# Attention scores as fp32 products of two heads side by side, in place of split float32r products

## The chip, the cores and the metric

The kernel runs on one core of one Trainium2 chip. The metric is the device time of one execution in microseconds, the median of three runs. TensorE, VectorE, ScalarE, GpSimd and SyncE are called PE, DVE, ACT, POOL and SP in the profile's rows; PEld is the weight load of PE.

## The reference

Two layers of a transformer trunk, on one sequence of 256 tokens with 1024 channels. Each layer takes shift, scale and gate from a condition vector, normalises, mixes, and adds the gated result to x. All matrices are float32.

```python
for i in range(2):
    shift, scale, gate = split(cond @ ada_w[i] + ada_b[i], 3)
    h = rms_norm(x, norm_g[i]) * (1 + scale) + shift
    x = x + gate * (nsa_mixer if i == 0 else moba_mixer)(h, ...)

# both mixers: 16 query heads of 64 channels, 4 key/value heads ("key groups"); query head h uses group h // 4
q, k.. = partial_rope(rms_norm(..., g))          # per head
# layer A (nsa): three attentions with the same q, each with keys of its own, mixed by per-head gates
o = g0 * softmax(q @ k_cmp.T * s) @ v_cmp        # 15 compressed keys a group
  + g1 * softmax(q @ k_sel.T * s) @ v_sel        # 256 tokens: at this length all blocks are selected
  + g2 * softmax(q @ k_win.T * s) @ v_win        # 256 tokens: at this length the window holds them all
# layer B (moba): one causal attention over 256 tokens
o = softmax(q @ k.T * s) @ v
return (o * silu(z)) @ w_out
```

## The kernel before, in words

**Products.** A float32 matrix that meets another in a large product is split in two float32r parts, `hi` (a rounding copy on ACT) and `lo` (a subtraction on DVE), and the product is the three matmuls hi·hi, hi·lo, lo·hi. This is done for the normalised input (`HT`), every projection weight (`parts_of`, tags `hi` and `lo`), and the gated attention output (`GT`, tag `qg`). The projections run in chunks of 512 columns: `piece` loads a quarter of the rows (128 partitions x 2 x 512) by one DMA on SP's queue into a `raw` buffer, `parts_of` splits it, `product` issues the matmuls. `z_blocks` does the same with the weight as the stationary side, so that the gate branch z comes out transposed.

**Scores.** They too were split. `make_k` normalises and rotates the keys, copies each head twice beside itself on ACT (`twice`, tag `y`), transposes the four key groups, and splits the transposed keys into `KTA[:, 0]` (hi) and `KTA[:, 1]` (lo). So each of the two parts has the 64 channels twice on its 128 partitions. `make_q` puts the hi and lo part of a head beside each other (`n_parts`), transposes that as float32r, and copies it to the query tile (`qg`): 64 partitions hi, 64 partitions lo. A score is then two matmuls with 128 contraction rows, against the hi keys and against the lo keys.

**Attention.** `pair_a(i)` and `pair_b(i)` handle two neighbouring heads, `e` = 0 and 1, that use one key group. For layer A a pair has three score blocks of 256 columns (tokens 0 to 127 against both kinds of keys, tokens 128 to 255 against each), for layer B one of 128 and one of 256 columns. DVE masks a block and takes the row maximum (`masked_top`), ACT takes the exponential with its sum (`exps`), DVE scales, PE transposes the probabilities (`p_transposed`), and `values` forms the outputs with two heads side by side in the columns of PE: 128 x 64 tiles, plain fp32 operands. `compressed(hf)` handles eight heads against 16 compressed keys each. Plain fp32 matmuls show as two records each in the trace.

**Tiles of PE.** A matmul with `tile_position` uses a part of the array. In the kernel before these are the 128 x 32 tiles of the condition products (`condz`), the 128 x 64 tiles of `values` and of the compression, the 32 x 128 tiles of `Vbd`, and one pair of 64 x 128 tiles, in `ada_gate(0)` (tile `row` against `ones`).

**Order.** Nothing is issued as it is written. Each engine call is recorded with an estimated duration, a tile pool and a level, and `Plan.issue` then simulates the engines and emits the calls engine by engine: the earliest call that can start, ties by level and by number. Numbers are moved by a table, `LATER_BY`; starts are held back by another, `HOLD`. `Plan._safe` says whether a tile may be taken ahead of its turn, `Plan._rank` prefers calls that keep PE in a tiled form. PSUM has eight banks: two `acc` and six `ps`; scores, transposes and outputs of the attention use `ps`. The projections of z in layer A, and the output products of a layer, are issued between the steps of the attention.

Of the kernel before, what the change touches and what calls it, by code (L numbers as in the profile page):

```python
# [9 lines left out]
F32 = mybir.dt.float32  # L10
# [47 lines left out]
    29: 2400, 32: 3700, 33: 3700, 51: 7200, 312: 35600, 391: 48800, 1276: 152700, 1340: 169100, 1350: 168000,  # L58
    1415: 182100, 1573: 197400, 1576: 198800, 1579: 197400, 1585: 198700, 1636: 205200, 1655: 209300,
# [13 lines left out]
class Plan:  # L73
# [120 lines left out]
    def _cost(self, engine, method, args, kw, aps):  # L194
# [15 lines left out]
        if engine == "T":  # L210
# [3 lines left out]
            if aps[2].dtype == F32:  # L214
                m, rows = free(aps[1]), aps[1].shape[0]
                if "tile_position" in kw and m * rows <= 64 * P:
                    return max(cols * 4.28 * max(32, m) / P * max(32, rows) / P, 60.0) + (100.0 if rows < P else 0.0)
# [25 lines left out]
    def _rank(op, e, mode):  # L243

        if e == "T" and op["level"] >= 0 and op["mode"] and mode:
            return TILED
# [1294 lines left out]
```

## Time and profile before

| | before |
|---|---|
| median of 3 runs | 312.29 us (312.12 to 313.19) |
| the profiled execution, its time | 312.48 us |
| its span | 310.7 us |
| PE busy | 301.6 us, 97% |
| PEld busy | 242.0 us, 78% |
| DVE busy | 242.0 us, 78% |
| ACT busy | 205.1 us, 66% |
| moved by DMA | 65.82 MB, mean 212 GB/s |

A matmul's record lasts from its start to the end of its pipeline, so neighbouring records overlap and the busy share is above what the array computes. What a matmul costs its neighbours is read from start to start. In a row of the timeline the first number is the start, the second the length of the whole row, and "x16" is the number of records merged in it; a row's cost is thus the next row's start minus its own. In a table of stages the columns are busy microseconds and records of PE, PEld, DVE, ACT and POOL, then PE's granted clock (1.00 is full), the DMA share and GB/s.

### The profile page before, as it was taken

The page shows a single profiled execution, that of the slowest core. Times are in us where ns is not written, and L with a number is a line of the kernel's source. Part 1 is how long each engine was busy: PE and PEld are TensorE (multiplying, and loading weights), DVE is VectorE, ACT ScalarE, POOL GpSimd, SP SyncE. Part 2 cuts the span into 40 slices and gives each one's busy share as a digit, 9 for nine tenths or more (in the row PEclk, how much of TensorE's full clock was granted, in tenths as well). Part 3 has the DMA queues.
Part 4 walks back from the last instruction along what each step waited for, and adds up shares of the span by engine and source line. Part 5 has one row for each costly group of instructions (what it writes and reads, how often), then busy time and mean ns, then how long its engine had stood idle before and what let it go on. Part 6 is the DMA issues. An engine that isn't in the chain of part 4 may idle for free.

```text
span 310.7 us, 6167 instructions
## 1 busy us (share of the span) xinstructions
PE 301.6 (97%) x2133; PEld 242.0 (78%) x2133; DVE 242.0 (78%) x734; ACT 205.1 (66%) x486; POOL 28.2 (9%) x99
## 2 busy tenths in 40 slices
PE   4999999999999999999999999999999999999995
PEld 4765677768767687976798887787788999987784
DVE  4763483658997399963999989796799999999465
ACT  4735254784845566964999993795585599988520
POOL 8038950000000000000000000000000000000000
PEclk9999999999999999999999999999999999999999
DMA  8999999749999890948925429236288760740002
GB/s 249 321 356 368 366 356 319 223 139 307 331 294 333 282 345 6 329 145 290 309 80 186 153 72 307 96 77 198 69 289 273 225 231 9 263 136 2 0 35 103
DMA packets 44174, 65.82 MB, mean 212 GB/s; under 512 B 4221, under 2 KB 20971, under 8 KB 44142
## 3 DMA queue, kind: packets, MB, share of 16 engines
q1 hardware_dynamic: 43782, 65.36, 64.3%
q8 instruction: 17, 0.28, 0.4%
q14 instruction: 15, 0.12, 0.1%
q10 hardware_dynamic: 168, 0.06, 0.1%
q0 software_dynamic: 192, 0.00, 0.0%
HBM read 64.36 MB, written 1.05 MB: 211 GB/s over the span
## 4 chain that ended last, share of the span: by engine, by line
PE 90%; DVE 3%; DMA 3%; ACT 2%; issue 1%; ACTq 0%; SPq 0%; DVEq 0%
PE ps L404 52%; PE acc L404 38%; DMA y<-in_ada_b_dram 2%; DMA early<-in_nsa_w_in_dram 1%; ACT hi L404 1%; DVE lo L404 1%; DVE rs L404 1%; DVE y L404 0%; ACT n_parts L404 0%; ACTq L404 0%; DVE X L404 0%; DVE p L404 0%; ACT n_out L404 0%; ACT HT L404 0%; DVE n_parts L404 0%
## 5 line engine op out<-in xcount | busy, mean ns | idle before, releaser
L404 ACT CAST hi<-raw 128x1024 fp32r<-128x1024 f32 (+1 forms) x48 | 48.6, 1021 | 24.3 <-PE acc L404 16.5
L404 DVE TENSOR_TENSOR lo<-raw,hi 128x1024 fp32r<-128x1024 f32 (+1 forms) x48 | 56.5, 1182 | 6.5 <-ACT hi L404 6.3
L404 PE MATMUL acc<-hi,HT 128*128 128x512 f32 (+1 forms) x160 | 49.6, 382 | 0.1
L404 ACT ACTIVATE p<-p,tiny 128x128 f32<-128x128 f32 (+1 forms) x96 | 42.9, 451 | 6.5 <-DVE tiny L404 6.2
L404 PE MATMUL acc<-HT,hi 128*128 128x256 f32 x192 | 37.4, 285 | 0.0
L404 DVE CUSTOM_DVE_ANT_0 p<-ps,causal 128x128 f32<-128x128 f32 (+1 forms) x96 | 30.6, 346 | 8.2 <-ACT hi L404 5.6
L404 PEld LDWEIGHTS acc<-hi,HT 128*128 128x128 f32 x160 | 29.1, 188 | 8.0 <-issue 2.5
L404 PEld LDWEIGHTS acc<-HT,hi 128*128 128x128 f32 x192 | 30.2, 189 | 0.5 <-issue 0.5
L404 PE MATMUL acc<-lo,HT 128*128 128x512 f32 (+1 forms) x80 | 30.3, 383 | 0.2
L404 PE MATMUL ps<-hi,HT 128*128 128x512 f32 (+1 forms) x96 | 28.2, 365 | 0.0
L404 PE MATMUL acc<-HT,lo 128*128 128x256 f32 x96 | 27.2, 284 | 0.0
L404 PE MATMUL ps<-KTA,qg 128*128 128x256 f32 (+2 forms) x192 | 26.9, 281 | 0.0
L404 PEld LDWEIGHTS ps<-KTA,qg 128*128 128x128 f32 x192 | 24.0, 189 | 2.7 <-issue 1.7
L404 ACT COPY pT<-ps 128x384 f32<-128x384 f32 x48 | 21.0, 477 | 4.0 <-PE ps L404 4.0
L404 ACT CAST hi<-early 128x1024 fp32r<-128x1024 f32 (+2 forms) x17 | 14.9, 896 | 13.1 <-DMA early<-in_nsa_w_in_dram 8.9
L404 PE MATMUL ps<-hi,qg 128*128 128x256 f32 (+1 forms) x96 | 23.4, 326 | 0.0
L404 DVE TENSOR_TENSOR lo<-early,hi 128x1024 fp32r<-128x1024 f32 (+2 forms) x17 | 17.6, 1047 | 5.9 <-ACT hi L404 5.9
L404 PE MATMUL acc<-hi,qg 128*128 128x512 f32 x64 | 21.7, 405 | 0.0
L404 PE MATMUL ps<-identF,p 128*128 128x128 f32 x144 | 21.2, 274 | 0.0
L404 PEld LDWEIGHTS ps<-hi,HT 128*128 128x128 f32 x96 | 17.0, 188 | 3.5 <-issue 1.2
L404 PEld LDWEIGHTS ps<-identF,p 128*128 128x128 f32 x144 | 16.8, 141 | 2.7 <-issue 0.7
L404 PE MATMUL ps<-pT,VA 128*64 128x256 f32 (+1 forms) x192 | 18.5, 333 | 0.0
(220 smaller groups left out, 614.4 us busy)
## 6 DMA issues: line engine op xcount, KB each, us to landing
raw<-in_ada_w_dram SPq DMA_DIRECT2D x32, 512.0 KB, 5.2
raw<-in_moba_w_in_dram SPq DMA_DIRECT2D x20, 512.0 KB, 4.4
early<-in_ada_w_dram SPq DMA_DIRECT2D x12, 512.0 KB, 9.5
raw<-in_nsa_w_in_dram SPq DMA_DIRECT2D x12, 512.0 KB, 6.8
early<-in_nsa_w_in_dram SPq DMA_DIRECT2D x9, 512.0 KB, 8.8
p<-in_nsa_cmp_w_dram SPq DMA_DIRECT2D x16, 256.0 KB, 4.1
raw<-in_nsa_w_out_dram SPq DMA_DIRECT2D x8, 512.0 KB, 4.8
raw<-in_moba_w_out_dram SPq DMA_DIRECT2D x8, 512.0 KB, 5.2
```

The lines of the kernel that those rows point to most:

```text
L404: r = getattr(self.engines[e], method)(*[self._real(a) for a in args], **{k: self._real(a) for k, a in kw.items()})
```

## The change

Queries and keys stay fp32 and have no low parts. The transposed key tile holds two key groups, one on partitions 0 to 63 and one on 64 to 127 (`KTA` is `[P, 2, 528]` fp32 in place of `[P, 2, 4, 528]` float32r), and the transposed query tile holds one head of each of these groups in the same way (tag `q`, two tiles). A score is one fp32 matmul with 64 contraction rows; the two heads of a pair stand one above the other in 64 x 128 tiles of PE and write two PSUM banks. So a pair's heads come from two key groups (heads j and j + 4 of a half of eight), and what goes by head is put in that order: the query projection's copies (`by_head`, `raw_part`), the gates, the z weights (`parts_of` with `paired`), the rows of the output weights (`out_piece`, two DMAs of 64 partitions in place of one of 128), the compressed values.

```diff
@@ scores
-        s = tile_of("ps", 2, 256)
-        with plan.group(need):
-            for e in range(2):
-                T.matmul(s[:, e, 0:n], q[e], kt[:, 0, g, k0:k0 + n], start=(e == 0), stop=False)
-                T.matmul(s[:, e, 0:n], q[e], kt[:, 1, g, k0:k0 + n], start=False, stop=(e == 1))
+        s = [tile_of("ps", sum(n for _, _, n in spans)) for e in range(2)]
+        at = 0
+        with plan.group(*needs):
+            for b, (m, k0, n) in enumerate(spans):
+                for e in range(2):
+                    half = slice(64 * e, 64 * e + 64)
+                    T.matmul(s[e][:, at:at + n], QT[i // 4][half, i % 4, m * P:(m + 1) * P], kt[half, i // 4, k0:k0 + n],
+                             start=(b == 0), stop=(b == len(spans) - 1), tile_position=(64 * e, 0))
+                at += n
@@ pair_a: scores(i, KTA, ((0, 128, 256),), p) and scores(i, KTA, ((1, 256, 256), (1, 0, 256)), *two)
@@ pair_b: scores(i, KTB, ((0, 0, P), (1, 0, S)), *pm)
@@ make_k
-            twice = tile_of("y", KVH, 2 * HD)
-            A.copy(twice.rearrange("p g (a d) -> p g a d", a=2),
-                   y[:, 4 * j:4 * j + 4, None, :].to_broadcast([P, KVH, 2, HD]))
-            t = tile_of("ps", 512)
+            t = tile_of("ps", 2, P)
             with plan.group():
-                for g in range(KVH):
-                    T.transpose(t[:, g * P:(g + 1) * P], twice[:, g], identF)
...
-            A.copy(hi, tv)
-            V.tensor_sub(lo, tv, hi.bitcast(F32))
+                for hf in range(2):
+                    T.transpose(t[:, hf], y[:, 4 * j + 2 * hf:4 * j + 2 * hf + 2].rearrange("p e d -> p (e d)"), identF)
+            A.copy(kt_view[:, :, off:off + P], t)
@@ make_q
-            qs = tile_of("n_parts", 8, 2, HD)
-            src = y[:, 8 * m:8 * m + 8]
-            A.copy(qs[:, :, 0, :], src)
-            V.tensor_sub(qs[:, :, 1, :], src, qs[:, :, 0, :].bitcast(F32))
-            for gg in range(2):
...
-                        T.transpose(t.bitcast(F32R)[:, h * P:(h + 1) * P],
-                                    qs[:, 4 * gg + h].rearrange("p a d -> p (a d)"), identR)
-                A.copy(qt[g0 + gg][:, :, m * P:(m + 1) * P], t.rearrange("p (h k) -> p h k", h=4))
+            t = tile_of("ps", 512)
+            with plan.group():
+                for h in range(4):
+                    T.transpose(t[:, h * P:(h + 1) * P],
+                                y[:, 8 * m + 2 * h:8 * m + 2 * h + 2].rearrange("p e d -> p (e d)"), identF)
+            A.copy(qt[g0 // 2][:, :, m * P:(m + 1) * P], t.rearrange("p (h k) -> p h k", h=4))
@@ compressed
-        s = tile_of("ps", 2, 8, 2, 16)
+        s = [tile_of("ps", 2, 4, 16) for e in range(2)]
...
-                    T.matmul(s[:, m, h], QT[g][:, h % 4, m * P:(m + 1) * P], KTA[:, :, g, 512:528],
-                             start=(m == 0 and h == 0), stop=(m == 1 and h == 7))
+                    half = slice(64 * (h % 2), 64 * (h % 2) + 64)
+                    T.matmul(s[h % 2][:, m, h // 2], QT[hf][half, h // 2, m * P:(m + 1) * P],
+                             KTA[half, hf, 512:528], start=(m == 0 and h < 2), stop=(m == 1 and h >= 6),
+                             tile_position=(64 * (h % 2), 0))
...
-        V.tensor_add(pc, s[:, :, :, 1], maskC[:, :, None, :].to_broadcast([P, 2, 8, 16]))
-        V.tensor_add(pc, s[:, :, :, 0], pc)
+        for e in range(2):
+            V.tensor_add(pc[:, :, e::2], s[e], maskC[:, :, None, :].to_broadcast([P, 2, 4, 16]))
@@ out_piece (new, in place of piece for the output weights)
+        with plan.at(CHAIN):
+            for e in range(2):
+                Q.dma_start(t[64 * e:64 * e + 64], bass.AP(tensor=w.tensor, offset=w.offset + (512 * hf + 256 * e + 64 * j) * D + c0,
+                                                           ap=[[D, 64], [64 * D, KP], [1, n]]))
@@ parts_of, paired (for z_blocks)
+                t = t.rearrange("p k (e j d) -> p (k e) j d", e=2, d=HD)
+                hv, lv = (h.rearrange("p k n -> p (k n)").rearrange("p (j c d) -> p c j d", j=4, d=HD) for h in (hi, lo))
@@ pools
-    plan.tag("n_parts", work, 1024, 2, F32R)
+    plan.tag("n_parts", work, 1024, 4, F32R)
-    ATTN = {"qg": (1024, 5, F32R), "zT": (512, 4, F32), "p": (512, 6, F32),
+    ATTN = {"qg": (1024, 4, F32R), "q": (1024, 2, F32), "zT": (512, 4, F32), "p": (512, 6, F32),
@@ first_parts: weight quarters of layer B's first chunk that are split before layer A ends
-        for kp in range(4):
+        for kp in range(3):
@@ Plan
-        if e == "T" and op["level"] >= 0 and op["mode"] and mode:
+        if e == "T" and op["level"] >= 0 and op["mode"] and mode == op["mode"]:
@@ LATER_BY: other numbers (63 entries before, 46 now); HOLD: other numbers (16 and 18 entries); in _safe another count of the tiles held
-    (162, 162, -17), (329, 337, -24), (338, 338, 30), (344, 351, -111), (359, 366, -38), (372, 372, -38),
+    (26, 27, 4), (102, 103, 904), (260, 260, 303), (276, 276, 13), (529, 529, -145), (576, 576, -37),
```

The counts that follow are of calls, and a plain fp32 matmul that is one call here has two records in a trace. PE had 64 float32r transposes of `n_parts` and 24 fp32 transposes of `y`, and now has 44 fp32 transposes of `n_out` (32 for queries, 12 for keys). The score matmuls were 128 of 256 columns, 32 of 128 and 32 of 32 columns; they are 64 of 256, 16 of 128 and 32 of 16 columns. The number of times that PE goes over from one tile form to another in its order of issue (full array, 128 x 32, 128 x 64, 32 x 128, 64 x 128) was 67 and is 103; the 64 x 128 form stood there once and now stands in 19 places.

PE, the first scores of layer B, before. `n_parts` are split queries, `KTA` holds the keys of layer B too, `qg` the query tiles, `HT,hi` is a product of the z projection.

```order
1050 L404 MATMUL ps_207<-identR,n_parts_1047 128x128 x4
1051 L404 MATMUL ps_242<-identR,n_parts_1047 128x128 x4
1052 L404 MATMUL ps_152<-identR,n_parts_1051 128x128 x4
1053 L404 MATMUL ps_215<-identR,n_parts_1051 128x128 x4
1054 L404 MATMUL ps_207<-KTA,qg_1080 128x128 x4
1055 L404 MATMUL ps_242<-KTA,qg_1080 128x128 x4
1056 L404 MATMUL ps_158<-HT,hi_332 128x256
1057 L404 MATMUL ps_152<-KTA,qg_1080 128x256 x4
```

The same place of PE now.

```order
1078 L401 MATMUL ps_198<-identF,n_out_271 128x128 x4
1079 L401 MATMUL ps_156<-identF,n_out_271 128x128 x4
1080 L401 MATMUL ps_150<-HT,hi_229 128x256
...
1086 L401 MATMUL ps_206<-HT,lo_358 128x256
1087 L401 MATMUL ps_234<-KTA,q_1020 128x128
1088 L401 MATMUL ps_245<-KTA,q_1020 128x128
1089 L401 MATMUL ps_234<-KTA,q_1020 128x256
1090 L401 MATMUL ps_245<-KTA,q_1020 128x256
1091 L401 MATMUL ps_198<-KTA,q_1020 128x128
```

Half of the transposes are gone, z products stand between them and the first scores, and a pair's scores are four calls in two banks where they were eight calls in two.

ACT, the same queries, before: the split, and the copies of four transposed heads each.

```order
265 L404 CAST n_parts_1047<-n_out_275 128x8x64
266 L404 CAST n_parts_1051<-n_out_275 128x8x64
...
269 L404 CAST qg_1080<-ps_207 128x4x128
270 L404 CAST qg_1091<-ps_242 128x4x128
271 L404 CAST qg_1080<-ps_152 128x4x128
272 L404 CAST qg_1091<-ps_215 128x4x128
```

ACT now, at that place and at the next query chunk of layer B.

```order
247 L401 COPY q_1020<-ps_198 128x4x128
248 L401 COPY q_1020<-ps_156 128x4x128
249 L401 CAST hi_229<-raw_662 128x4x4x64
...
261 L401 COPY pT_1278<-ps_156 128x384
262 L401 COPY q_1360<-ps_245 128x4x128
263 L401 COPY q_1360<-ps_150 128x4x128
```

Six ACT calls became two (row 249 is a weight split in the new order of heads, row 261 a copy of transposed probabilities); the two subtractions on DVE that stood between are gone as well.

More of the change, by code (lines that the diff above doesn't have):

```diff
@@ L236, in _safe @@
             tag.known[k] = all(
-                sum(a not in held and a not in tag.done for a in tag.alive[b]) + len(held) <= tag.bufs
+                sum(a not in tag.done for a in tag.alive[b]) + sum(h > b for h in held) <= tag.bufs
                 for b in range(tag.next, len(tag.tiles)) if b not in held and b not in tag.given and tag.first[b] <= end)
@@ L562 @@
     nc.gpsimd.memset(ones, 1.0)
-    identR = const.tile([P, P], F32R, name="identR")
-    V.tensor_copy(identR, identF)
     emask = const.tile([P, 2], F32, name="emask")
@@ L938, in values @@
                 for e in range(2):
-                    T.matmul(o[64 * e:64 * e + 64, 0:S], v[0], pT[e][:, 0:S], start=(first and n == 0), stop=False,
+                    T.matmul(o[64 * e:64 * e + 64, 0:S], v[0][e], pT[e][:, 0:S], start=(first and n == 0), stop=False,
                              tile_position=(0, 64 * e))
                 for e in range(2):
-                    T.matmul(o[64 * e:64 * e + 64, P:S], v[1], pT[e][:, S:S + P], start=False,
+                    T.matmul(o[64 * e:64 * e + 64, P:S], v[1][e], pT[e][:, S:S + P], start=False,
                              stop=(n == len(parts) - 1), tile_position=(0, 64 * e))
@@ L1034 @@
     kv_acc.append([q_acc[:, m] for m in range(2)])
-    KTA = const.tile([P, 2, KVH, 528], F32R, name="KTA")
+    KTA = const.tile([P, 2, 528], F32, name="KTA")
     VA = const.tile([P, 2, 2, 256], F32, name="VA")
@@ L1262 @@
     norm_rope(kcm[:, None, 0:64], 1, 1, TCc[:, None, :], TSc[:, None, :], kcy)
-    kcs = tile_of("n_parts", 1, 2, 2, HD)[0:64]
-    both = kcy[:, :, None, :].to_broadcast([64, 1, 2, HD])
-    V.tensor_copy(kcs[:, :, 0], both)
-    V.tensor_sub(kcs[:, :, 1], both, kcs[:, :, 0].bitcast(F32))
+    kcs = tile_of("rot", 2, HD)[0:64]
+    V.tensor_copy(kcs, kcy[:, 0, None, :].to_broadcast([64, 2, HD]))
     tk = tile_of("ps", 512)
-    with plan.group():
-        for part in range(2):
-            T.transpose(tk.bitcast(F32R)[:, part * 64:part * 64 + 64],
-                        kcs[:, 0, part].rearrange("p a d -> p (a d)"), identR[0:64, 0:64])
-    A.copy(KTA[:, :, :, 512:528], tk[:, 0:128].rearrange("p (a g n) -> p a g n", a=2, g=KVH))
+    T.transpose(tk[:, 0:64], kcs.rearrange("p a d -> p (a d)"), identF[0:64, 0:64])
+    for e in range(2):
+        A.copy(KTA[64 * e:64 * e + 64, :, 512:528],
+               tk[64 * e:64 * e + 64, 0:64].rearrange("p (f e n) -> p f e n", f=2, e=2)[:, :, e])
     vb = tile_of("ps", 512)
@@ L1325, in pair_a @@
     def pair_a(i):
[L1326 removed]
+        hf, j_ = i // 4, i % 4
         ps = []
         neg, sm = tile_of("tiny", 2, 2, 2), tile_of("tiny", 2, 2, 2)
[L1329 to L1342 removed]
+        for m in range(2):
+            if m == 0:
+                p = tile_of("p", 2, 2, P)
+                s = scores(i, KTA, ((0, 128, 256),), p)
+                blocks = [(p[:, e, r], s[e][:, r * P:(r + 1) * P], e, r, 0) for e in range(2) for r in range(2)]
+                ps.append(p)
+            else:
+                two = [tile_of("p", 2, 1, S) for _ in range(2)]
+                s = scores(i, KTA, ((1, 256, 256), (1, 0, 256)), *two)
+                blocks = [(two[1 - r][:, e, 0], s[e][:, (1 - r) * S:(2 - r) * S], e, r, P * r) for r in (1, 0) for e in range(2)]
+                ps += two
+            for dst, src, e, r, at in blocks:
+                masked_top(dst, src, neg[:, m, e, r:r + 1], at)
+            for dst, src, e, r, at in blocks:
+                exps(dst, neg[:, m, e, r:r + 1], sm[:, m, e, r:r + 1])
         smf = sm.rearrange("p m e r -> p (m e r)")
@@ L1368, in pair_a @@
         o = ov[hf, j_]
-        vs = slice(g * HD, (g + 1) * HD)
-        values(o, [([VA[:, m, 1 - r, vs] for m in range(2)], pT[r]) for r in (1, 0)], False)
+        vs = [slice((2 * (i // 4) + e) * HD, (2 * (i // 4) + e + 1) * HD) for e in range(2)]
+        values(o, [([[VA[:, m, 1 - r, v] for v in vs] for m in range(2)], pT[r]) for r in (1, 0)], False)
         gated(i, o, zT[i])
@@ L1482, in pair_b @@
         neg, sm = tile_of("tiny", 2, 2), tile_of("tiny", 2, 2)
+        s = scores(i, KTB, ((0, 0, P), (1, 0, S)), *pm)
         for m in range(2):
             n = P * (m + 1)
-            q = [QT[g][:, 2 * (i % 2) + e, m * P:(m + 1) * P] for e in range(2)]
-            s = scores(q, KTB, g, 0, n, pm[m])
             for e in range(2):
-                masked_top(pm[m][:, e], s[:, e, 0:n], neg[:, m, e:e + 1], m * P)
+                masked_top(pm[m][:, e], s[e][:, P * m:P * m + n], neg[:, m, e:e + 1], m * P)
             for e in range(2):
@@ L1496, in pair_b @@
         o = tile_of("ps", 512)
-        vs = slice(g * HD, (g + 1) * HD)
-        values(o, [([VB[:, m, vs] for m in range(2)], pT)], True)
+        vs = [slice((2 * (i // 4) + e) * HD, (2 * (i // 4) + e + 1) * HD) for e in range(2)]
+        values(o, [([[VB[:, m, v] for v in vs] for m in range(2)], pT)], True)
         gated(i, o, zT[i])
```

80 lines of the change are left out of this document (33 added, 47 removed), and 18 rows, old and new, of the table LATER_BY.

## The prediction

> **What bounds the kernel now.** I read the page's shares first, then the chain, then the table of stages.
>
> ```profile
> PE 301.6 (97%) x2133; PEld 242.0 (78%) x2133; DVE 242.0 (78%) x734; ACT 205.1 (66%) x486; POOL 28.2 (9%) x99
> ...
> PE 90%; DVE 3%; DMA 3%; ACT 2%; issue 1%; ACTq 0%; SPq 0%; DVEq 0%
> ```
>
> PE is busy for 97% of the span and is 90% of the chain that ended last. The stages show where others come near it.
>
> ```profile
> 150.00:160.00 10.00, 9.99 (x88) 9.20 (x88) 10.00 (x50) 9.72 (x32) 0.00 (x0) 1.00 0.67 210
> 170.00:180.00 10.00, 10.00 (x73) 8.35 (x73) 10.00 (x44) 9.69 (x34) 0.00 (x0) 1.00 0.44 144
> 180.00:190.00 10.00, 10.00 (x78) 8.00 (x77) 8.58 (x17) 7.88 (x18) 0.00 (x0) 1.00 0.50 137
> 200.00:210.00 10.00, 9.74 (x50) 7.73 (x48) 9.27 (x23) 8.96 (x23) 0.00 (x0) 1.00 0.26 68
> 240.00:250.00 10.00, 9.74 (x90) 9.54 (x88) 10.00 (x18) 5.95 (x9) 0.00 (x0) 1.00 0.80 263
> 250.00:260.00 10.00, 10.00 (x91) 10.00 (x90) 10.00 (x47) 9.47 (x27) 0.00 (x0) 1.00 0.36 118
> 270.00:280.00 10.00, 10.00 (x79) 8.51 (x77) 10.00 (x43) 8.53 (x29) 0.00 (x0) 1.00 0.41 132
> ```
>
> PE never rests in the attention, at full clock; DVE is full there too and ACT nearly. PE can fill because projections stand ready between the attention's steps, so the time follows the sum of PE's work, as long as DVE, which is as full, is not given more. The change must be priced in PE's start-to-start time first.
>
> **Transposes of queries and keys.** This is the safest term.
>
> ```profile
> 125.83 1.85 PE L404 MATMUL ps<-KTA,qg 128*128 128x32 f32 x16
> 127.53 1.56 PE L404 MATMUL ps<-identR,n_parts 128*128 128x128 f32 x16
> 128.92 0.62 PE L404 MATMUL ps<-identF,row 128*128 128x128 f32 x4
> ...
> 268.44 0.56 PE L404 MATMUL ps<-KTA,qg 128*128 128x128 f32 x4
> 268.83 1.49 PE L404 MATMUL ps<-identF,p 128*128 128x128 f32 x12
> 270.08 0.64 PE L404 MATMUL ps<-KTA,qg 128*128 128x128 f32 x4
> 270.65 2.37 PE L404 MATMUL ps<-pT,VA 128*64 128x256 f32 x24
> 272.95 2.13 PE L404 MATMUL ps<-KTA,qg 128*128 128x256 f32 x16
> 274.92 0.28 PE L404 MATMUL acc<-HT,hi 128*128 128x256 f32 x1
> ```
>
> Sixteen float32r transposes took 128.92 - 127.53 = 1.39 us, 87 ns each; twelve fp32 ones 270.08 - 268.83 = 1.25 us, 104 ns each. Before: 64 x 0.087 + 24 x 0.104 = 8.1 us. After: 44 x 0.104 = 4.6 us. PE saves 3.5 us.
>
> **Scores, before.**
>
> ```profile
> 152.34 1.70 PE L404 MATMUL ps<-KTA,qg 128*128 128x256 f32 x12
> 153.96 1.52 PE L404 MATMUL ps<-pT,VA 128*64 128x256 f32 x16
> 155.41 1.22 PE L404 MATMUL ps<-KTA,qg 128*128 128x256 f32 x8
> ```
>
> Twelve matmuls, one pair of layer A, took 1.62 us: 8 pairs, 13.0 us. In layer B, the 16 from 272.95 took 1.97 us (123 ns each) and four of 128 columns 0.39 us (98 ns each), so a pair of 4 + 4 takes about 0.93 us: 8 pairs, 7.4 us. The compressed scores took 1.70 us for 16 (106 ns each), twice: 3.4 us. Together 23.8 us.
>
> **Scores, after.** No score in this trace is fp32 in 64-row tiles, but one operation has the form exactly (`row,ones`, 64 x 128), and two heads side by side in columns have the same arithmetic.
>
> ```profile
> 107.52 0.28 PE L404 MATMUL acc<-HT,lo 128*128 128x256 f32 x1
> 107.63 0.39 PE L404 MATMUL acc<-HT,hi 128*128 128x256 f32 x2
> 107.95 1.08 PE L404 MATMUL ps<-p,p 128*64 128x256 f32 x8
> 108.97 1.13 PE L404 MATMUL ps<-row,ones 64*128 64x512 f32 x4
> 110.03 0.44 PE L404 MATMUL ps<-identF,g 128*128 128x128 f32 x2
> ```
>
> `row,ones` is two matmuls of 512 columns, one in each half, each in two records: 1.06 us for both. `p,p` streams 512 columns through two side-by-side tiles in 1.02 us, and the sixteen records of `values` at 153.96 stream 2 x 256 + 2 x 128 = 768 in 1.45 us. The difference is 0.43 us for 256 columns: 1.68 us for 1000 columns of two heads, and about 0.16 to 0.20 us for the group as such. So the halves do run at once. Streaming alone then gives for layer A 768 columns a pair, 1.29 us x 8 = 10.3 us; for layer B 384 columns, 0.645 x 8 = 5.2 us.
>
> Going into a tiled form and out again also costs. The group's own surplus is 0.16 to 0.20 us; and the two full matmuls ahead of `p,p` took 0.32 us where two take 2 x 0.11 (107.63 - 107.52), so 0.10 us more is lost there. A visit costs 0.26 to 0.30 us, 0.14 us per change of form. The order of issue has 36 changes more: 36 x 0.14 = 5.0 us.
>
> A rule of the Trainium skill (TensorEngine Tiling (Array Packing), Key Properties) speaks against the change here: going over to another tiling mode drains the array, while going on to another tile of the same mode does not. A full drain would be a lone matmul's whole latency less its normal step, by the rows above 0.28 - 0.11 = 0.17 us, and 36 x 0.17 = 6.1 us in place of 5.0: by the rule the sum below is 1.1 us higher. The trace shows the loss, at 0.14 us a change somewhat smaller than a full drain, and I keep the rows' value.
>
> The compressed scores become 16 matmuls of 16 columns for each half of the heads, 32 records with 32 weight loads; what they stream is nothing, so the loads and the issue set the pace. The bounds:
>
> ```profile
> L404 PEld LDWEIGHTS ps<-KTA,qg 128*128 128x128 f32 x192 | 24.0, 189 | 2.7 <-issue 1.7 <-ACT row L404 0.8 <-ACT pT L404 0.2
> ...
> L404 PEld LDWEIGHTS ps<-row,ones 64*128 64x128 f32 x4 | 0.3, 184 | 0.4 <-ACT p L404 0.4
> ```
>
> A 64-row load lasts 184 ns, like a 128-row load with 189. If the loads go one after another at the step of the full ones (106 ns a record, above), a half takes 3.4 us, two 6.8. But the four loads of `row,ones` are over in 0.30 us in all, so they start 39 ns apart, in alternating halves: 32 x 0.039 = 1.25 us, two 2.5. I take half the full step, 53 ns, 1.7 us a half, 3.4 in all, since two halves alternate here as well, without the long streams of `row,ones`; 2.5 and 6.8 stay as ends.
>
> Sum of the scores after: 10.3 + 5.2 + 3.4 + 5.0 = 23.9 us, against 23.8. The arithmetic is the same, 1024 column steps for two heads and 256 keys; what layer B's short blocks gain, the changes of form take. So PE's whole gain is that of the transposes, 3.5 us.
>
> **Work of DVE and ACT.** Both get less, in the stages where they are full.
>
> ```profile
> L404 ACT CAST hi<-early 128x512 fp32r<-128x512 f32 x5 | 3.1, 627 | 1.8 <-issue 1.8
> L404 ACT CAST qg<-ps 128x512 fp32r<-128x512 f32 x16 | 8.2, 599 | 1.2 <-PE ps L404 1.2
> L404 ACT CAST n_parts<-n_out 128x512 fp32r<-128x512 f32 x8 | 4.6, 621 | 0.1
> L404 ACT COPY y<-n_out 128x512 f32<-128x512 f32 x6 | 3.4, 619 | 0.8 <-DVE n_out L404 0.8
> L404 ACT CAST KTA<-ps 128x512 fp32r<-128x512 f32 x6 | 3.2, 585 | 0.1
> L404 ACT COPY n_in<-ps 128x256 f32<-128x256 f32 x4 | 1.5, 377 | 0.0
> L404 DVE TENSOR_TENSOR n_parts<-n_out,n_parts 128x512 fp32r<-128x512 f32 x8 | 5.1, 682 | 0.0
> L404 DVE TENSOR_TENSOR KTA<-ps,KTA 128x512 fp32r<-128x512 f32 x6 | 3.9, 681 | 0.0
> L404 DVE TENSOR_TENSOR pc<-ps,maskC 128x256 f32<-128x256 f32 x2 | 0.8, 421 | 0.0
> L404 DVE TENSOR_TENSOR Vbd<-ps,emask 128x128 f32<-128x128 f32 x2 | 0.5, 270 | 0.0
> ```
>
> DVE loses 8 x 0.682 + 6 x 0.681 = 9.5 us of subtractions; of the compressed scores four additions of 0.42 become four of half the size, 0.27 each, 0.6 us less. ACT loses 8 x 0.621 + 6 x 0.619 = 8.7 us, and 8 of 16 copies at 0.599, and six copies get half as long (0.585 to about 0.377): 14.7 us. Neither is on the path that ends the kernel while PE is full, so this only pays where PE waits: in the table of stages PE lacks 0.26 us in 200 to 210 and 0.26 us in 240 to 250. A PE that seems full may also be held inside its overlapping records. Bounds: 0, and, taking those two stages' losses for each of the some four stages where DVE is full, 1 us. I take 0.6 us.
>
> **What costs nothing, and its cover.** The split of the z weights in the new order reads and writes runs of 64. `n_parts` was written in runs of 64 and took 621 ns where the plain split of the same size took 627, so runs of 64 are free. The query copies in runs of 64 and two gate calls more on DVE are hidden likewise. The output weights come in 16 DMAs more on SP; their landing is covered by buffers ahead, at a DMA share of 0.44 to 0.50 from 170 to 190. If that cover were gone, a late quarter would show as PE waiting for `lo`. The one weight quarter that is no longer split ahead of layer B stands in the normal queue, and at 200 to 210, where PE would meet it, ACT has a tenth of its time free.
>
> **Sum.** 312.48 - 3.5 (transposes) + 0.1 (scores) - 0.6 (waits) = 308.5 in terms of the profiled execution, which lies 0.19 above the median of 312.29; so 308.3 us. With all ends on the good side (compressed scores -0.9, changes at 0.08 us a change, the groups' own surplus alone, -2.1, waits -0.4) it is 304.9; with all on the bad side (+3.4, drains +1.1, waits +0.6) it is 313.4.
>
> **Rivals.**
>
> 1. The compressed scores are bound by their weight loads. For it: 184 against 189 ns for a load, whatever its rows. Against it: 39 ns between the loads of `row,ones`. It costs 6.8 - 3.4 = 3.4 us: 311.7, within 0.5% of before (a measurement of this kernel tells no less than about that from no change). The Trainium skill (TensorE: Matmul & The Clock Gate, LDWEIGHTS) says the same: a load's time goes by columns, and a 32 x 128 load takes as long as a 128 x 128 load. The durations agree; whether loads of two halves overlap is what decides.
>
> 2. PSUM: a pair of layer A now holds four of the six `ps` banks with scores in place of three, and the second group frees its first bank only after DVE has masked three of its blocks. If DVE, full at 150 to 180 and 250 to 280, is late, the next pair's transposes find no bank and PE stands. Price: one masked block of 256 columns, of the order of the 0.42 us of the 256-column DVE row above, for each of 16 pairs, 6.7 us, so 315.0: slower. It decides from 0.33 us a pair on, where 5.4 us are lost and 313.8 is passed. Against it: the projections write to `acc` as well and can fill.
>
> 3. The two halves do not run at once for scores, against what `row,ones` shows: 15.5 us more, 323.8.
>
> 4. It gains more than the sum: the lighter DVE and ACT let the attention of both layers run denser, where both were full. Ten of the some 25 us that they lose, passed on at half, are 5 us: 303.5.
>
> **How the numbers follow.** Forecast 0.56 (304.9 to 310.7, faster). Rival 1, 0.13 (same). Rival 2, 0.13: 0.04 same, 0.09 slower. Rival 3, 0.04, slower. Rival 4, 0.14, faster. So faster 0.70, same 0.17, slower 0.13. The range leaves out rivals 2 (slower) and 3 and about half of rival 4: 303.5 to 312.5.
>
> **What would show it.** In the changed kernel: records `ps<-KTA,q` of 64 x 128 whose starts in the timeline give 1.3 us plus 0.5 of changes for a pair of layer A; the 32 records of a half's compressed scores in some 1.7 us; 44 transposes of `n_out` at 104 ns; DVE near 232 and ACT near 190 us busy; PE busy some 4 us less. Wrong: a compressed half of 3.4 us (rival 1); waits of PE or PEld on DVE `p` or `tiny` in 150 to 180 (rival 2); a pair above 2.6 us (rival 3); full stages much shorter than the PE terms account for (rival 4).

## The result: 0.8% slower

The changed kernel takes 315.66 us (median of 15 runs), the kernel before, on the same chip, 312.76 us (15 runs): ratio 1.0084, 95% interval 1.0066 to 1.0101. The profiled execution took 316.31 us with a span of 314.6 us. Below, each run has a ratio to the kernel before on the same chip, and microseconds are worked out from it: 0.001 is 0.31 us, and the changed kernel's 0.0084 is +2.6 us. A ratio's interval is about 0.0025 to either side, so two ratios that lie within some 0.003 are not told apart. (The two medians alone give 1.0093; the ratio comes from all runs.)

The page of the changed kernel: shares, then the chain.

```profile
PE 304.5 (97%) x2120; PEld 235.0 (75%) x2120; DVE 234.2 (74%) x720; ACT 194.1 (62%) x465; POOL 29.6 (9%) x99
...
PE 92%; DMA 3%; DVE 2%; ACT 2%; issue 0%; ACTq 0%; DVEq 0%
```

DVE and ACT lost 7.8 and 11.0 us, three quarters of what was forecast (10.1 and 14.7); PE, which was to lose 4, is busy 2.9 us longer. The stages (columns as before):

```profile
150.00:160.00 10.00, 10.00 (x86) 7.70 (x88) 8.64 (x49) 9.73 (x38) 0.00 (x0) 1.00 0.21 80
200.00:210.00 10.00, 10.00 (x51) 7.64 (x50) 8.43 (x25) 8.63 (x22) 0.00 (x0) 1.00 0.33 108
250.00:260.00 10.00, 10.00 (x88) 8.97 (x87) 10.00 (x38) 7.06 (x23) 0.00 (x0) 1.00 0.87 264
270.00:280.00 10.00, 10.00 (x91) 8.72 (x90) 10.00 (x40) 9.07 (x30) 0.00 (x0) 1.00 0.42 110
```

PE is full in 200 to 210 now, where it lacked 0.26. At 150 to 160, in layer A, DVE has room (8.64, where it was at 10.00), ACT has as little as before (9.73 and 9.72). In layer B DVE still has none. The timeline gives the terms of the sum:

```profile
84.20 1.09 PE L401 MATMUL ps<-identF,n_out 128*128 128x128 f32 x8
85.22 1.08 PE L401 MATMUL ps<-p,p 128*64 128x256 f32 x8
...
121.33 1.96 PE L401 MATMUL ps<-KTA,q 64*128 64x16 f32 x32
123.22 0.39 PE L401 MATMUL acc<-HT,lo 128*128 128x256 f32 x1
...
134.71 1.57 PE L401 MATMUL ps<-KTA,q 64*128 64x256 f32 x12
136.21 1.09 PE L401 MATMUL ps<-pT,VA 128*64 128x256 f32 x10
```

Eight transposes take 1.02 us, with the change of form behind them; over the trace 44 average 110 ns, where 104 were forecast. A half's compressed scores take 1.89 us. Twelve records of a pair's scores take 1.50 us.

Added from each PE record's start to the next one's over the whole trace (us, before and after):

| PE's time goes to | before | after | difference |
|---|---|---|---|
| transposes of queries and keys | 8.30 | 4.85 | -3.45 |
| scores | 23.64 | 22.81 | -0.83 |
| z products | 47.38 | 50.70 | +3.32 |
| first projections, both layers | 96.29 | 97.80 | +1.51 |
| transposes of probabilities | 13.55 | 15.55 | +2.00 |
| output products | 47.91 | 45.95 | -1.96 |
| start (to the end of the last `n_in` transpose of layer A) | 12.57 | 14.29 | +1.72 |
| all else | 57.46 | 59.07 | +1.61 |
| sum | 307.10 | 311.02 | +3.92 |

The two rows that the change is about fall by 4.3 us. What takes longer is work that the change does not touch; z and the projections have the same number of matmuls before and after. (About half of +2.00 and -1.96 belong together: where an output product follows a transpose, some 0.08 us are booked on the one or the other, and there are 3 such places where there were 15. Another 0.9 us of the +2.00 are the last transposes ahead of scores: five at 0.20 us, where three took 0.03. The start is not steady: with the same order of PE's calls there, the first product comes at 12.68 us in one run below and at 14.65 in another.)

### The profile page after: what moved, and what is told of

Same layout as the page of the kernel before. It is cut to its first block, busy times and chain, and to the rows that moved or that the text cites. A ratio compares the mean times of both kernels' runs of the same rounds, so it can differ in the third digit from the quotient of the medians.

```text
span 314.6 us, 6134 instructions
## 1 busy us (share of the span) xinstructions
PE 304.5 (97%) x2120; PEld 235.0 (75%) x2120; DVE 234.2 (74%) x720; ACT 194.1 (62%) x465; POOL 29.6 (9%) x99
## 3 DMA queue, kind: packets, MB, share of 16 engines
HBM read 64.36 MB, written 1.05 MB: 208 GB/s over the span
## 4 chain that ended last, share of the span: by engine, by line
PE 92%; DMA 3%; DVE 2%; ACT 2%; issue 0%; ACTq 0%; DVEq 0%
PE ps L401 53%; PE acc L401 39%; DMA early<-in_ada_w_dram 1%; DMA y<-in_norm_g_dram 1%; DVE lo L401 1%; ACT hi L401 1%; ACT p L401 0%; DVE n_in L401 0%; DVE n_out L401 0%; ACT zT L401 0%; DVE rot L401 0%; DVE p L401 0%; ACTq L401 0%; ACT HT L401 0%; DVE y L401 0%
## 5 line engine op out<-in xcount | busy, mean ns | idle before, releaser
L401 PE MATMUL acc<-hi,HT 128*128 128x512 f32 (+1 forms) x168 | 53.5, 385 | 0.4 <-DVE tiny L401 0.4
L401 ACT ACTIVATE p<-p,tiny 128x256 f32<-128x256 f32 (+1 forms) x96 | 42.6, 448 | 10.1 <-DVE tiny L401 10.0
L401 PE MATMUL acc<-HT,hi 128*128 128x256 f32 x192 | 39.0, 290 | 0.0
L401 PEld LDWEIGHTS acc<-hi,HT 128*128 128x128 f32 x168 | 30.6, 188 | 9.5 <-issue 2.8
L401 DVE CUSTOM_DVE_ANT_0 p<-ps,causal 128x256 f32<-128x256 f32 (+1 forms) x96 | 30.1, 352 | 8.0 <-PE ps L401 7.7
L401 PE MATMUL acc<-lo,HT 128*128 128x512 f32 (+1 forms) x84 | 32.2, 383 | 0.2 <-DVE lo L401 0.2
L401 PE MATMUL ps<-KTA,q 64*128 64x256 f32 (+2 forms) x224 | 24.1, 343 | 0.0
L401 PEld LDWEIGHTS ps<-KTA,q 64*128 64x128 f32 x224 | 16.8, 186 | 3.5 <-issue 0.9
L401 PEld LDWEIGHTS acc<-HT,lo 128*128 128x128 f32 x96 | 18.0, 188 | 1.4 <-issue 1.2
L401 PEld LDWEIGHTS acc<-lo,HT 128*128 128x128 f32 x84 | 15.8, 188 | 4.1 <-DVE lo L401 0.8
```

Source lines behind the costliest of these rows:

```text
L401: r = getattr(self.engines[e], method)(*[self._real(a) for a in args], **{k: self._real(a) for k, a in kw.items()})
```

## The experiments

Where a kernel leaves out part of the computation, its expectation says which. "Order unchanged" means that every engine issues its calls in the same sequence.

**Start.** One hold of the new table (`43: 5100`) keeps back an input scaling; in the trace of the changed kernel the condition products now stand ahead of the first transposes:

```profile
10.05 1.94 PE L401 MATMUL ps<-early,condz 128*32 128x128 f32 x32 [1.77 <-DMA early<-in_ada_w_dram]
11.92 1.12 PE L401 MATMUL ps<-identF,n_in 128*128 128x128 f32 x4
```

```diff
-    37: 10300, 43: 5100, 130: 16800, ...
+    37: 10300, 130: 16800, ...
```

> One entry of the table HOLD is taken out of the changed kernel (43: 5100, the second row-square of x on ACT); in every engine's order only calls of the first 25 us move: the scaling of the second token half comes ahead of the first weight split on ACT, and PE transposes x ahead of the condition products. Theory 1, the start is a loss of its own: the first product comes at about 12.6 us as before and not at 14.3, and the kernel gains 1.4 to 1.7 us, 314.1. Rival: the DMA stream that feeds the first 60 us sets their end, later slack swallows it, and the time stays at 315.7.

Measured 1.0063 (1.0039 to 1.0086), so -0.65 us. The second run puts all calls of the first 45 us in the order of the kernel before.

> The changed kernel with the calls that the kernel before issues in its first 45 us (all engines, the 14 displaced loads of SP among them) put in that kernel's order; every later call stays as in the changed kernel. The trace of the changed kernel has its first product of the key and value chunks 3.5 us later than before (70.48 against 66.93 us), and PE's unexplained time in the first 20 us is 2.2 us higher. Theory start: 2 to 3.5 us of the loss are this order and stay gained to the end: 312.2 to 313.7. Theory attention: the time is set by PE's work and form changes from 80 us on, and what the start loses is slack that comes back: 315 to 315.7, like the one hold taken out (315.1).

Measured 1.0070 (1.0050 to 1.0090), so -0.4 us. The transposes now come at 8.57 (a kernel whose order is written out has other line numbers):

```profile
8.57 1.09 PE L506 MATMUL ps<-identF,n_in 128*128 128x128 f32 x4
9.59 1.17 PE L506 MATMUL ps<-early,condz 128*32 128x128 f32 x32
```

Neither is told from zero by its interval. So the start is worth some half a microsecond, not 2 to 3.5.

**Scores in another form.** One full-array fp32 matmul for both heads in place of the pair of 64 x 128 tiles, order unchanged; the second head's scores are left out.

```diff
-                for e in range(2):
-                    T.matmul(s[e][:, at:at + n], QT[i // 4][half, ...], kt[half, ...], tile_position=(64 * e, 0))
+                T.matmul(s[1][:, at:at + n], QT[i // 4][:, i % 4, ...], kt[:, i // 4, k0:k0 + n])
```

> Same order of calls on all engines as the changed kernel, but a pair's scores are one fp32 matmul on the full array (128 rows, both heads summed; the second head's own scores are left out), which streams just as long as the two side by side, without a change of tile form. 16 visits of the 64 x 128 form go, 32 changes. Theory 1, every change costs a full drain of 0.17 us: 5.4 us less, 310.2. With the 0.14 us of the prediction: 4.5 us less, 311.2. Rival, PSUM and DVE hold the attention (banks held, blocks late) and not the changes of form: 315 or more, since those waits stay as they are.

Measured 1.0045 (1.0019 to 1.0072), -1.2 us, a third of the expected. The same place in the changed kernel, then in this one, shows why:

```profile
107.00 0.40 PE L401 MATMUL acc<-HT,hi 128*128 128x256 f32 x2
107.33 1.13 PE L401 MATMUL ps<-KTA,q 64*128 64x256 f32 x8
108.39 0.38 PE L401 MATMUL acc<-HT,lo 128*128 128x256 f32 x1
108.61 0.40 PE L401 MATMUL acc<-HT,hi 128*128 128x256 f32 x2
```

```profile
105.47 0.40 PE L401 MATMUL acc<-HT,hi 128*128 128x256 f32 x2
105.71 1.02 PE L401 MATMUL ps<-KTA,q 128*128 128x256 f32 x4
106.38 0.47 PE L401 MATMUL acc<-HT,lo 128*128 128x256 f32 x1
106.69 0.40 PE L401 MATMUL acc<-HT,hi 128*128 128x256 f32 x2
```

In the tiled form the two z steps ahead take 0.33 us, 0.10 more than 2 x 0.117, and the first behind takes 0.22, 0.10 more. In the full form nothing is paid ahead. The step behind takes 0.31, but the group's own rows are that much shorter: 0.67 us, where four records at 0.216 (their step inside such a group) are 0.86; 0.67 and the 0.19 more of the step behind are just these 0.86. So the full form loses nothing here, and the tiled visit costs 0.40 us more (0.10 ahead, 1.06 - 0.86 in its own rows, 0.10 behind). Over the trace scores and z together fall by only 1.55 us, for part of the gain is lost in waits that the changed kernel does not have, such as this one:

```profile
167.18 1.13 PE L401 MATMUL ps<-KTA,q 128*128 128x256 f32 x4 [0.86 <-ACT pT L401]
```

**Compressed scores.** Keys block-diagonal, one full-array fp32 matmul of 32 columns for both heads.

```diff
-                    T.matmul(s[h % 2][:, m, h // 2], QT[hf][half, ...], KTA[half, hf, 512:528], tile_position=(64 * (h % 2), 0))
+                    T.matmul(s[:, m, j], QT[hf][:, j, m * P:(m + 1) * P], KD[:, hf])
```

> Same order of calls, but the compressed keys of two groups stand in a block-diagonal tile (32 columns with zeros), so a pair's compressed scores are one fp32 matmul on the full array: 16 records a half in place of 32, and no visit of the 64 x 128 form. Theory 1: 1.89 us a half becomes 16 x 0.106 = 1.7, and two visits of 0.34 us go: 1.0 us less, 314.6. Rival, the compressed scores lie beside waits for DVE that come anyway: 315.7.

Measured 1.0047 (1.0024 to 1.0071), -1.2 us with an interval of some 0.9 about it, but the rows show only 0.19 us for this half (1.70 against 1.89):

```profile
121.50 1.87 PE L401 MATMUL ps<-KD,q 128*128 128x32 f32 x16
123.20 0.37 PE L401 MATMUL acc<-HT,lo 128*128 128x256 f32 x1
```

Sixteen records with full loads take nearly as long as 32 with half ones. What the interval leaves beyond these rows is not explained.

**Without tables.** Both kernels with `LATER_BY` and `HOLD` empty.

> The changed kernel with both tables, LATER_BY and HOLD, empty: every call in the order that the planner's rules give. Theory 1 has part of the loss in the new tables: if they were worth nothing, 315 to 317. If the tables of the changed kernel are worth what such tables usually are for, several us more: 320 or above.

> The kernel before with both tables empty (no call moved, none held back). The changed kernel without its tables took 326.4. Theory order: the tables hide how well each kernel's work fits; the change as such, under the bare rules, is worse by far more than 0.8%, so this kernel comes out well under 326, 313 to 319. Theory work: what the change costs is the same with and without tables, 2.5 to 4 us, so this one takes about 322 to 324.

Measured 1.0416 (1.0367 to 1.0466) and 1.0081 (1.0054 to 1.0108). The tables are worth 2.5 us to the kernel before and 10.4 us to the changed one. Under the bare rules the change costs far more, so it fits the order of calls less well; which calls are to blame this does not say. (The bare rules are not quite the same in both: the change alters lines of `Plan`, and these were not tried alone.)

**Less for ACT and DVE.** Both kernels, order unchanged.

```diff
-        A.activation(dst, dst, AF.Exp, bias=bias, scale=-1.0, accum_out=total)
+        A.activation(dst[:, 0:32], dst[:, 0:32], AF.Exp, bias=bias, scale=-1.0, accum_out=total)
```

> The changed kernel with its order of calls written out call by call, and with less for ACT and DVE in the attention: the exponentials of a score block on 32 of its 128 or 256 columns, the scaling of layer A's probabilities on 32 columns, no causal mask (and a floor under the sums); so the probabilities are not the reference's. PE's work is the same. ACT loses some 24 us, DVE some 8. Theory waits: PE is held by banks that ACT and DVE free late, the growth of ACT's and DVE's waits on PE being the other side of it; then the time falls by 2 us or more and by at least 1.5 us more than in the kernel before. Theory PE: the sum of PE's own work and form changes sets the time; it falls by under 1 us, to 314.7 or more, and the two kernels change alike.

> The same lightening in the kernel before, order written out call by call, the same parts left out. Theory waits: it gains less than the changed kernel does, under 1 us, 312 or more. Theory PE: it gains as little as the changed kernel, under 1 us. If the kernel before gains more than the changed one, its attention was the denser of the two and the lighter ACT and DVE of the change found no use.

Measured 1.0089 (1.0059 to 1.0119) and 0.9967 (0.9952 to 0.9982). The two pages' shares:

```profile
PE 302.6 (97%) x2120; PEld 233.5 (75%) x2120; DVE 228.6 (73%) x728; ACT 183.4 (59%) x465; POOL 28.9 (9%) x98
```

```profile
PE 300.8 (97%) x2133; PEld 241.9 (78%) x2133; DVE 237.1 (77%) x742; ACT 195.7 (63%) x486; POOL 27.4 (9%) x98
```

ACT lost 11 us rather than 24, as a short activation still takes 316 ns. The changed kernel gains nothing (0.9 us at most, by the intervals), the kernel before 1.0 us. So ACT's exponentials and DVE's scaling, as far as they were shortened, are not what slows the changed kernel; rival 2's masking on DVE was left in place, and the run does not test it.

**Place of the buffers.** An unused tile behind the constants moves every work buffer; order unchanged.

```diff
     Vbd = const.tile([P, 2, P], F32, name="Vbd")
+    pad = const.tile([P, 32], F32, name="pad")
```

> The changed kernel with one unused tile of 128 bytes a partition behind its constants, so that every work buffer (hi, lo, raw, qg and the rest) lies 128 bytes further up; the order of calls is the same, HT stays. In the records a float32r step of z takes 117.5 ns in every version of the changed kernel and 114.5 in every version of the kernel before, a step of 512 columns of the first chunks 233.3 and 229.8, whatever the order and the time. By the programs' address maps hi and lo start at byte 64 of a 256-byte block in the changed kernel and at byte 192 before, qg the other way round. Theory place: that offset sets the step; z falls to 114 to 115, the 512-column steps to 229 to 230.5, and with 384 and some 300 of them the kernel gains 1.5 to 2.3 us: 313.3 to 314.2. Theory content: the slower steps come from something else in the program; nothing moves, 315.4 to 316.

> The kernel before with the same unused tile of 128 bytes; hi and lo go from byte 192 to byte 64 of a 256-byte block, order unchanged. Theory place: z goes to 117 to 118 ns, the 512-column steps to 233, and the kernel loses 1.5 to 2.3 us: 314.3 to 315.1. Theory content: 312.5 to 313.1, no change.

Measured 1.0053 (1.0034 to 1.0072), -1.0 us, and 1.0024 (1.0004 to 1.0045), +0.75 us. The same 92 z products in the kernel before and in its shifted copy, first and last row of each:

```profile
237.85 0.28 PE L404 MATMUL ps<-HT,hi 128*128 128x256 f32 x1
...
248.19 0.28 PE L404 MATMUL ps<-HT,lo 128*128 128x256 f32 x1
```

```profile
239.73 0.28 PE L404 MATMUL ps<-HT,hi 128*128 128x256 f32 x1
...
250.45 0.28 PE L404 MATMUL ps<-HT,lo 128*128 128x256 f32 x1
```

10.34 and 10.72 us: 113.6 and 117.8 ns a step. In the changed kernel, 30 first-projection steps of layer B fell with the shift from 7.00 us to 6.88; its z steps only partly (117.5 to 116.5 on average). Its longest run of z, 66 products, still takes 117.7 ns a step:

```profile
242.45 0.28 PE L401 MATMUL ps<-HT,hi 128*128 128x256 f32 x1
...
250.22 0.42 PE L401 MATMUL ps<-identF,n_out 128*128 128x128 f32 x2
```

So the place is shown as a cause in the kernel before and for the projections; for most of z in the changed kernel, whose weights are also split in a new order, the longer step stays open. Two more places:

> The changed kernel with an unused tile of 192 bytes instead: hi and lo start at a 256-byte boundary, qg at byte 128. Theory place gives no certain sign here; if the step grows with the parts into which a row of 512 or 1024 bytes is cut, it is the fastest of the three, z at 113 or less and the time 313 or less. Theory content: 315.4 to 316.

> The changed kernel with an unused tile of 64 bytes: hi and lo start at byte 128 of a 256-byte block, where HT stands in all of them. Theory place: between the offsets 64 and 192 or beyond one of them, z at 113 to 118; 313 to 316. Theory content: 315.4 to 316.

Measured 1.0058 (1.0036 to 1.0081) and 1.0064 (1.0042 to 1.0085): z steps of 118.6 and 119.9 ns, and projection steps of 232.7 and 229.2. Of the places tried, byte 192, where the kernel before has `hi` and `lo`, is the only one at which neither grows.

**Float32r scores in the changed order.** As in the kernel before, two float32r matmuls a block and head; order unchanged.

```diff
-                    T.matmul(s[e][:, at:at + n], QT[i // 4][half, ...], kt[half, ...], tile_position=(64 * e, 0))
+                    for part in range(2):
+                        T.matmul(s[e][:, at:at + n], QT[i // 4][:, i % 4, ...], kt[:, i // 4, ...])   # float32r
```

> The changed kernel, order of calls written out and unchanged, with a pair's scores as before on PE: float32r on the full array, two matmuls a block and head, keys and queries rounded to float32r (each score is then twice the sum over both heads, so the output is not the reference's); the compressed scores stay in 64 x 128 tiles. The arithmetic time of the scores stays about the same (12 x 256 columns a pair of layer A in 1.62 us). Theory neighbours: what the fp32 scores cost lies in the changes of kind: 0.10 us more for a z step ahead of them, 0.11 for the first behind, 0.17 for a last transpose ahead (0.20 where it took 0.03 ahead of a float32r score), and some 0.2 in their own rows; with 16 visits gone the kernel gains 2.5 to 4.5 us: 311.2 to 313.2. Theory order: these steps are long because of where the calls stand; PE's scores alone change, by +0.5 to +1: 315.7 to 316.7.

Measured 1.0036 (1.0008 to 1.0063), -1.5 us, short of the 2.5 expected. The place shown above, with float32r scores:

```profile
106.26 0.40 PE L506 MATMUL acc<-HT,hi 128*128 128x256 f32 x2
106.50 1.21 PE L506 MATMUL ps<-KTA,q 128*128 128x256 f32 x8
107.55 0.28 PE L506 MATMUL acc<-HT,lo 128*128 128x256 f32 x1
107.66 0.40 PE L506 MATMUL acc<-HT,hi 128*128 128x256 f32 x2
```

The scores take 1.05 us as against 1.06; the z steps beside them 0.24 and 0.11 as against 0.33 and 0.22. The visit's price at its neighbours, 0.20 us here, is gone. Over the trace the scores' own rows grew by 1.3 us, z fell by 1.5 and the transposes of probabilities by 0.7.

**fp32 scores in the order of before.**

```diff
-                T.matmul(s[:, e, 0:n], q[e], kt[:, 0, g, k0:k0 + n], start=(e == 0), stop=False)
-                T.matmul(s[:, e, 0:n], q[e], kt[:, 1, g, k0:k0 + n], start=False, stop=(e == 1))
+                T.matmul(s[:, e, 0:n], q[e].bitcast(F32), kt[:, 0, g, k0:k0 + n].bitcast(F32), start=(e == 0), stop=(e == 1))
```

> The kernel before, order of calls written out and unchanged, with one plain fp32 matmul on the full array in place of the two float32r matmuls of each block and head (the products with the low parts of the keys are left out, so the output differs from the reference's); the arithmetic time is the same, 2 x 256 columns. Theory neighbours: the last transposes ahead of a score go from 0.03 to 0.13 us or more, the first float32r step behind from 0.12 to 0.31, so the some 40 score groups, most of them in runs of their own, lose 3 to 6 us: 316 to 319. Theory order: the kind of the scores costs its neighbours nothing, 312.5 to 313.5.

Measured 1.0345 (1.0308 to 1.0383), +10.8 us, beyond both theories, since my arithmetic was wrong:

```profile
105.36 1.99 PE L508 MATMUL ps<-KTA,qg 128*128 128x256 f32 x8
107.00 0.59 PE L508 MATMUL acc<-HT,hi 128*128 128x256 f32 x2
```

A full-array fp32 record of 256 columns takes 216 ns from start to start inside its groups, twice what I had assumed. The scores' own rows grew by 9.95 us, z by 1.7, the transposes of probabilities by 0.2. What it does show is that work added to PE here is paid in full. The 0.19 us more of the step behind are again what the group's last record is short of.

**All causes together.** Float32r scores, start of before, buffers 128 bytes up; then the block-diagonal compressed scores too.

> The kernel of the run with float32r scores, with the start of the kernel before (first 45 us) and the work buffers 128 bytes further up as well; output not the reference's for the same reason. If the causes add: 0.3 to 0.5 us less for the start and 0.7 to 1 for the place than the run with float32r scores alone. Theory neighbours: 309.8 to 312. Theory order: 314.3 to 315.5.

> The changed kernel with all four measured costs taken out together: float32r scores on the full array (output not the reference's, each score is twice the sum over both heads), compressed scores as full-array products with block-diagonal keys, the start of the kernel before, work buffers 128 bytes further up. By addition from the run without the block-diagonal keys (ratio 1.0017): 0.3 to 1.2 us less, 312.2 to 313.1, ratio 0.998 to 1.001. Against the kernel before it then has the same kinds of work on PE and 3.3 us of transposes less; if the order of calls cost nothing, it would be at 309 to 310, ratio 0.988 to 0.991.

Measured 1.0017 (0.9995 to 1.0038) and 1.0030 (1.0010 to 1.0050): the last part adds nothing. With its costs taken out, the changed kernel comes within 0.5 to 0.9 us of the kernel before, but not below it, although its transposes take 3.3 us less (4.97 against 8.30). By the rows of the second run against the kernel before, z takes 1.6 us more, the first projections 0.8 more, and the products `p,p` and `pcT,Vbd`, which make and use the compressed keys and values, 1.2 more. Some 0.9 of z's 1.6 are its step, 116.7 ns here and 114.4 there; why the rest is longer is open, and the order of the calls, which differs, is a rival. The mended kernel, with its fp32 scores kept:

> The changed kernel with its fp32 scores in 64 x 128 tiles kept, and three things mended: the start of the kernel before, the work buffers 128 bytes further up, and the compressed keys of a head pair block-diagonal in a tile of their own, so that one full-array fp32 matmul gives both heads' 32 scores. If the single effects (0.4, 0.7 to 1 and 0.5 to 1.2) add: 313.0 to 314.0, at best even with the kernel before. If they overlap, because each only moves a wait, 314 to 315.

Measured 1.0040 (1.0019 to 1.0062), 1.4 us better than the changed kernel, and still behind the kernel before. The effects do not simply add.

**Does saved PE work pay at all?** The kernel before, order unchanged, with 24 of its 64 query transposes left out.

```diff
-                    for h in range(4):
+                    for h in range(4 if gg == 0 else 1):
```

> The kernel before, order of calls written out and unchanged, with 24 of its 64 float32r query transposes left out (of every second group of four only one is made, and its copy to the query tile reads the group before it, so half of the query tiles hold other heads' values). 24 x 87 ns are 2.1 us of PE. Theory sum, as in the prediction: PE never rests in the attention, so the time follows its work: 310.4 to 311.2, ratio 0.992 to 0.995. Theory order: PE's stream is held together by its waits on ACT and DVE at other places, and the saving is lost: 312.2 or more, ratio 0.998 to 1.

Measured 0.9996 (0.9976 to 1.0016): 0.1 us of 2.1, and by the interval at most 0.75 (the two medians, 312.38 and 313.01, lie 0.6 apart). Over the trace the rows of the query and key transposes fall by only 1.1 us, since PE now waits inside them. The timeline shows a saving and its loss. In the kernel before the 16 transposes at 127.53 are followed by others at 128.92 and by 9 records from 129.38 to 130.28 (0.90 us). Here:

```profile
127.53 1.05 PE L508 MATMUL ps<-identR,n_parts 128*128 128x128 f32 x10
128.41 0.63 PE L508 MATMUL ps<-identF,row 128*128 128x128 f32 x4
128.88 1.48 PE L508 MATMUL ps<-identF,p 128*128 128x128 f32 x9
130.11 0.72 PE L508 MATMUL ps<-KTA,qg 128*128 128x256 f32 x4
```

PE is 0.51 us ahead at 128.41; the 9 transposes of probabilities then take 1.23 us. The chain of this stretch, first in the kernel before, then here (start, us, what):

```profile
125.99 5.01 PE ps L404 x49
```

```profile
126.49 0.49 ACT pT L508
126.98 1.48 ACT p L508 x6
128.46 0.97 ACT qg L508 x2
129.43 0.04 issue
129.48 1.35 PE ps L508 x10
```

The chain goes over to ACT, whose exponentials and query copies were just behind PE. In layer B the same, at the first scores, which come 0.13 us later than in the kernel before (250.13):

```profile
248.56 1.23 PE L508 MATMUL ps<-identR,n_parts 128*128 128x128 f32 x10 [0.26 <-DVE n_parts L508]
250.26 1.00 PE L508 MATMUL ps<-KTA,qg 128*128 128x128 f32 x7 [0.47 <-ACT qg L508]
```

The profiled execution has one loss that is not the saving's: at 86.71, ahead of the first transpose left out (96.48), the eight `p,p` records take 1.51 us where they took 1.01; what they wait for the trace does not name. It eats what the first six transposes save. By 133 us PE is 0.05 us ahead of the kernel before, at the end not at all.

## Why the prediction was wrong

**The step that failed: "so the time follows the sum of PE's work".** The work added to the kernel before came through in full (+10.8 us), the work saved did not. The saving of 3.5 us was sized rightly (3.45), but of 2.1 us taken out of the kernel before alone, 0.1 arrived, 0.75 at most; there the chain went over to ACT, only tenths of a microsecond behind PE. In the changed kernel the 3.3 us were not seen either once its costs were out. So a PE that is busy for 10.00 of 10 us can be held inside its overlapping records by another engine. I named that possibility, and used it only as a bound for the 0.6 us. It is not a rule for every saving: the shorter projection steps of the shifted kernel did arrive (1.0 us). And the run with fewer transposes left ACT and DVE their work, of which the change took 11.0 and 7.8 us; that the transposes bring nothing in the changed kernel too is inferred, not shown.

**Scores, forecast +0.1 us.** Their own rows took 22.81 us, where I had 23.9 with the changes of form in it. I had the own surplus of a visit and 0.10 us ahead of it; the 0.10 to 0.11 that the first float32r step behind pays I left out. With all three a visit costs some 0.4 us, 0.2 a change in place of 0.14. The streaming itself was right (1.29 us a pair, and six pairs of records at 0.216). The Trainium skill (TensorEngine Tiling (Array Packing), Key Properties) says that changing the tiling mode drains the array; the 0.17 us a change that I had worked out for such a drain from the rows was nearer. A compressed half took 1.89 us where 1.7 was forecast. Together with the neighbours the scores cost 1.5 us (0.5 to 2.5) more than float32r ones, by the run that put those back.

**Waits, forecast -0.6 us.** PE did get the missing 0.26 us in 200 to 210, but no gain is seen: another 11 us less on ACT brought the changed kernel nothing.

**Not in the sum.** The new place of the buffers, 0.75 and 1.0 us by the two shifts; the start, 0.4 to 0.65 us (neither told from zero).

**The account.** +1.5 (scores) + 0.9 (place) + 0.5 (start) + 0 (transposes) + 0 (waits) = +2.9 us against +2.6 measured (2.1 to 3.2). Its parts have intervals of about 0.9 us each, and the mended kernel shows that they overlap; that the sum comes out so near is partly luck.

**Rivals.** 1: a compressed half at 1.89 us is far from 3.4; it fell. 2: slower was right and 315.0 near; its sign, waits for DVE `p` or `tiny` in 150 to 180, is there, but only once each, and of the weight loads alone:

```profile
PEld ps L401 <- DVE p L401: 0.8, 1, 0.8
PEld ps L401 <- DVE tiny L401: 0.2, 1, 0.2
```

PE itself waits for neither there. That is far from 0.42 us for each of 16 pairs, but the masking was not tried alone. 3: a pair's twelve records take 1.50 us, so the halves do overlap. 4: fell; the kernel is slower, and ACT and DVE made lighter still brought nothing.

**Open.** The tables are worth 10.4 us to the changed kernel. Whether a better order for it exists is not settled; no order tried here beat the kernel before. Not tried alone were the new order of the z weights, the 16 more DMAs of the output weights, the weight quarter that is split later, and fewer transposes together with lighter ACT and DVE in the kernel before.

## What to carry to other kernels

Before pricing a saving on a full engine, take the work out of the old kernel alone, order unchanged, and see whether the time moves: in a tuned schedule other engines can stand just behind, and then additions count in full and a saving may hardly count. Price a new kind of matmul at its neighbours too, ahead and behind, since a group's own rows can get shorter while the products beside it get longer. Count a group together with the step behind it, for a record's rest can be booked there. And when untouched work is slower everywhere by the same share, compare where its operands lie.

## What the runs showed of the hardware

- A float32r step of 256 columns has two levels, 113.6 and 117.8 ns at full clock. In the kernel before, moving the work buffers by 128 bytes changed the one into the other; in the changed kernel the move back did so for a part of the z steps only.
- Between float32r products and fp32 tiles of 64 rows PE loses 0.10 us ahead, 0.20 in the group and 0.10 to 0.11 behind. Between float32r products and full-array fp32 it loses nothing: what the step behind is longer (0.19), the group's last record is shorter. A float32r score costs its neighbours nothing.
- A full-array fp32 matmul of 256 columns is two records of 216 ns, as against 114 ns for a float32r one. Two fp32 tiles of 64 rows, one above the other, take the same 216 ns for a record of each.
